# Keys and values of heads 4 to 7 projected in pairs; gates' logits split between VectorE and ScalarE

## The chip, the cores and the metric

The kernel runs on one core of a Trainium2 chip. The metric is the device time of one execution in microseconds (us), smaller is better. Besides the times there is one profiled execution, whose trace records every instruction of the engines: PE (TensorE, with its weight loads as PEld), DVE (VectorE), ACT (ScalarE), POOL (GpSimd), and SP, which only issues DMAs.

## The reference

One step of a decoder layer for 512 prompt tokens behind 16 meta tokens, and for 32 sample tokens (8 sequences of 4) that have 512 past keys and values each in a paged cache. All data are float32.

```python
h = rmsnorm(x, g_pre)
q, k, v, ga, cb, cc, ch, gc, ma, mc = jnp.split(h @ w_in, split_offsets(), axis=-1)
a = attend(q, k, v, b_sb) * jax.nn.silu(ga)          # 8 heads of 128, strictly causal
c = cb * causal_conv(cc * ch, w_conv, b_conv) * jax.nn.silu(gc)
m = jax.nn.sigmoid(ma + b_gate[:D]) * (a @ w_pa) + jax.nn.sigmoid(mc + b_gate[D:]) * (c @ w_pc)
y = x + rmsnorm(m @ w_out, g_post)
# attend: z = q.k / sqrt(128) + b;  A[t,s] = sigmoid(z_ts) * prod over s<j<t of (1 - sigmoid(z_tj))
```

The outputs also hold all keys, values and the convolution's last rows.

## The kernel before, in words

**Numbers in two parts.** Each float32 matrix is split into a part cast to the type fp32r and the rest (`hi`, `lo`), and each product is three matmuls: hi·hi, hi·lo, lo·hi. For weights ACT makes the cast (`whi`, line 240) and DVE subtracts it (`wlo`, line 241), 128x1024 at a time. A weight tile `raw` is one 512 KB load, issued by SP into five buffers; whi and wlo have three.

**Tokens.** 560 tokens (528 of the prompt with meta, 32 of the sample) lie along the free dimension of `h_hi`, `h_lo`, in two halves of 280 columns (272 where meta tokens aren't needed, 274 in the convolution's inputs).

**Two ways to project.** `proj` (line 271, its matmuls on line 256) takes one block of 128 output columns: 16 blocks of the contraction, three matmuls each, for both halves. `pair` with `seven` (lines 974 to 1024, matmuls on line 971) takes two blocks of output columns at once as a 2x2 block product with seven products of 8 blocks in place of eight. It needs sums of weight blocks (`s`, `w21`, on DVE), sums of token blocks (`t_hi`, `t_lo` 0 to 2, and `r1`, written over the block of h in the upper contraction half and second token half), and differences of partial results (`s2`, `s5`, `c`). Single projections that read h whole must come before that overwriting.

**The order.** Normalization and the first four queries; `head_now` for heads 0 to 3 (K, V, a query projection of head 4 to 7, and the prompt's attention); `head_later` for heads 4 to 7 (K and V by single projections, kept in DRAM for attention later); the block sums; then pairs: 4 for the attention's gate GA, 16 for the convolution (four groups of CC, CH, GC, CB), 16 for the gates MA and MC; then the products with w_pc with the attention of heads 4 to 7, with w_pa, and with w_out.

**The decode.** A generator, `decode_steps` (line 759), is advanced by `dec_step` and holds the sample's attention over the cache. Its first phase makes the logits: 16 units (half of the heads, sequence), each with two loads of query rows, broadcast to all partitions (`qb`, 512 KB), and four pages of keys (`kpage`, 256 KB), issued by POOL. A page takes 16 reduces on DVE, a product of 128 elements summed into one column of `z_all` each (line 781), 4 tokens by 4 heads. The first 6 units (`DEC1`) are spread over heads 0 to 7 ("part"), the other 10 over the first 25 pairs ("logits"), a step of `dec_group` (line 900) behind each pair being one page in the convolution and up to four in the gates. Then come the softplus and the sums over positions (`dec2`), and the values' pages in the last pairs.

**Who sets the order.** The tile framework schedules each engine's instructions by a simulated timeline with the program's order as priority, puts in the semaphores, and keeps the order of those that are marked (`pin`). Each engine then runs its own list strictly in order. Pools marked `side="right"` share one stack of SBUF, which bounds what can be held at once.

Of the kernel before, what the change touches and what calls it, by code (L numbers as in the profile page):

```python
# [17 lines left out]
P = 128  # L18
# [29 lines left out]
DEC1 = 6  # L48
# [12 lines left out]
def hybrid_step_kernel(  # L61
# [499 lines left out]
    def k_proj(h):  # L561
        o = proj(GATE_K + h * P, ALL)
        kr = hp.tile([P, T], F32, name="raw", bufs=2)
        for ob, s in nparts(o):
            act.copy(kr[:, s], ob)
# [11 lines left out]
    def v_proj(h, pl=None):  # L577
        o = proj(GATE_V + h * P, ALL)
        vr = hp.tile([P, T], F32, name="raw", bufs=2)
        for ob, s in nparts(o):  # L580
            act.copy(vr[:, s], ob)
# [5 lines left out]
        if pl is None:  # L587
            pool.dma_start(vn_scr[h][0:512].rearrange("(a p) d -> p a d", p=P), vn[:, 0:4, :])
            pool.dma_start(vn_scr[h][512:TP], vn[0:16, 4, :])
            return None  # L590
        return v_split(pl, vn)
# [126 lines left out]
    def head_now(h):  # L718
# [40 lines left out]
    def decode_steps():  # L759
# [3 lines left out]
        for said, part in (("part", units[:DEC1]), ("logits", units[DEC1:])):  # L763
            with tc.tile_pool(name="dec1", bufs=2, side="right") as d1:
                for hf, b in part:
# [3 lines left out]
                    for i in range(2):  # L769
                        qt = d1.tile([P, 2, 512], F32, name="qb", bufs=3)  # L770
# [3 lines left out]
                    for pg in range(NPG):  # L774
                        kt = d1.tile([P, 512], F32, name="kpage", bufs=3)
                        first(page_load(kt, kc, b, pg, cs))
                        for i, qt in enumerate(qts):
                            for t in range(2):
                                for h in range(4):
                                    junk = d1.tile([P, P], F32, name="junk", bufs=2)  # L780
                                    dve.tensor_tensor_reduce(  # L781
# [716 lines left out]
```

## Time and profile before

| | us |
|---|---|
| median of 3 runs (lowest to highest) | 1584.69 (1582.47 to 1585.42) |
| the profiled execution's own time | 1584.74 |
| its span, from the first instruction to the last | 1583.1 |
| single projections on line 256, share of the chain that ended last | 27.3% |
| pairs on line 971, share of that chain (into mm, into o) | 32.0%, 23.6% |

In the views that follow, "x" stands before a count, "mean ns" is the duration of one instruction with whatever it overlaps, and "idle before" the time in which its engine stood before it with the releaser named. Matmuls overlap: their durations are longer than the time from one to the next. The granted clock is TensorE's, as a share of full speed.

### The profile page before, as it was taken

The numbers are of one execution on the slowest core, as the hardware profiler recorded it, in microseconds if no ns is written. First come the engines' busy times: TensorE is split into PE (matmuls) and PEld (weight loads), VectorE is DVE, ScalarE is ACT, GpSimd is POOL, SyncE is SP. The second block draws the span as 40 slices with busy tenths as digits, with TensorE's granted clock in tenths as the row PEclk, the third lists the DMA queues.
The fourth block names the chain that finished last, engine by engine and source line by source line (L and its number), as shares of the span: only waits on it lengthen the run. The fifth ranks groups of instructions, "written<-read, shape, count | busy, mean of one in ns | idle before, by whom it ended". The sixth has DMA issues, their size and how long they took to land.

```text
span 1583.1 us, 32334 instructions
## 1 busy us (share of the span) xinstructions
PE 1560.7 (99%) x12172; PEld 1527.5 (96%) x12172; DVE 1268.5 (80%) x3574; ACT 761.7 (48%) x1345; POOL 234.7 (15%) x428
## 2 busy tenths in 40 slices
PE   8999999999999999999999999999999999999997
PEld 7999999999999999999999999898899999999997
DVE  7329999956799999999999997565678857877776
ACT  6245555435444444444444457444476734345552
POOL 1123333222111010011011102312100010000000
PEclk9999999999999999999999999999999999999999
DMA  8245556344454544445465545767595455433345
GB/s 263 82 137 186 168 160 184 107 130 136 150 180 124 151 130 140 146 134 162 120 181 173 162 138 168 245 194 226 157 306 172 148 178 165 152 107 94 101 143 183
DMA packets 300674, 252.77 MB, mean 160 GB/s; under 512 B 11521, under 2 KB 268613, under 8 KB 299701
## 3 DMA queue, kind: packets, MB, share of 16 engines
q1 hardware_dynamic: 272021, 160.45, 35.1%
q0 software_dynamic: 28368, 89.98, 17.0%
q8 instruction: 95, 1.56, 0.4%
q14 instruction: 62, 0.51, 0.1%
q10 hardware_dynamic: 128, 0.27, 0.1%
HBM read 217.95 MB, written 32.71 MB: 158 GB/s over the span
## 4 chain that ended last, share of the span: by engine, by line
PE 94%; DVE 2%; ACT 1%; DMA 1%; issue 1%; DVEq 0%; SPq 0%; ACTq 0%
PE mm L971 32%; PE mm L256 27%; PE o L971 24%; PE mm L321 2%; PE z L702 1%; PE o L714 1%; PE z L321 1%; PE tp L856 1%; DMA raw<-in_w_in 1%; PE z L620 1%; PE z L1439 1%; PE tp L505 0%; PE z L1293 0%; DVE wlo L241 0%; DMA at<-a_scr 0%
## 5 line engine op out<-in xcount | busy, mean ns | idle before, releaser
L240 ACT CAST whi<-raw 128x1024 fp32r<-128x1024 f32 x247 | 259.4, 1051 | 375.5 <-PE mm L971 135.0
L241 DVE TENSOR_TENSOR wlo<-raw,whi 128x1024 fp32r<-128x1024 f32 x247 | 301.7, 1222 | 90.2 <-ACT whi L240 88.0
L971 PE MATMUL mm<-h_hi,whi 128*128 128x272 f32 (+1 forms) x1152 | 333.5, 289 | 0.7 <-ACT whi L240 0.7
L971 PE MATMUL mm<-h_hi,wlo 128*128 128x272 f32 (+1 forms) x1152 | 332.6, 290 | 0.0
L971 PE MATMUL mm<-h_lo,whi 128*128 128x272 f32 (+1 forms) x1152 | 332.5, 289 | 0.0
L971 PE MATMUL o<-t_hi,whi 128*128 128x272 f32 (+1 forms) x864 | 251.6, 291 | 3.3 <-DVE c L997 3.3
L971 PE MATMUL o<-t_lo,whi 128*128 128x272 f32 (+1 forms) x864 | 251.2, 291 | 0.0
L971 PE MATMUL o<-t_hi,wlo 128*128 128x272 f32 (+1 forms) x864 | 251.1, 291 | 0.0
L781 DVE CUSTOM_DVE_ANT_0 junk<-kpage,qb 128x128 f32<-128x128 f32 x1024 | 246.0, 287 | 4.0 <-DMA qb<-q_scr 3.7
L971 PEld LDWEIGHTS mm<-h_hi,whi 128*128 128x128 f32 x1152 | 217.4, 189 | 6.1 <-ACT whi L240 3.5
L971 PEld LDWEIGHTS mm<-h_lo,whi 128*128 128x128 f32 x1152 | 216.8, 188 | 0.9 <-issue 0.8
L971 PEld LDWEIGHTS mm<-h_hi,wlo 128*128 128x128 f32 x1152 | 217.0, 189 | 0.2
L240 ACT CAST whi<-s 128x1024 fp32r<-128x1024 f32 x126 | 132.0, 1048 | 151.2 <-PE mm L971 48.5
L241 DVE TENSOR_TENSOR wlo<-s,whi 128x1024 fp32r<-128x1024 f32 x126 | 154.2, 1224 | 62.8 <-ACT whi L240 61.3
L256 PE MATMUL mm<-h_lo,whi 128*128 128x280 f32 (+1 forms) x640 | 187.6, 293 | 0.0
L256 PE MATMUL mm<-h_hi,wlo 128*128 128x280 f32 (+1 forms) x640 | 187.1, 293 | 0.0
L256 PE MATMUL mm<-h_hi,whi 128*128 128x280 f32 (+1 forms) x640 | 186.7, 292 | 0.0
L971 PEld LDWEIGHTS o<-t_hi,whi 128*128 128x128 f32 x864 | 164.1, 190 | 4.0 <-DVE c L997 4.0
L971 PEld LDWEIGHTS o<-t_hi,wlo 128*128 128x128 f32 x864 | 164.5, 190 | 0.9 <-issue 0.8
L971 PEld LDWEIGHTS o<-t_lo,whi 128*128 128x128 f32 x864 | 164.8, 191 | 0.0
L256 PEld LDWEIGHTS mm<-h_lo,whi 128*128 128x128 f32 x640 | 120.3, 188 | 0.8
L256 PEld LDWEIGHTS mm<-h_hi,wlo 128*128 128x128 f32 x640 | 120.5, 188 | 0.5
(452 smaller groups left out, 3166.7 us busy)
## 6 DMA issues: line engine op xcount, KB each, us to landing
raw<-in_w_in SPq DMA_DIRECT2D x192, 512.0 KB, 4.5
kpage<-in_cache_k POOLq DMA_DIRECT2D x64, 256.0 KB, 3.8
qb<-q_scr POOLq DMA_DIRECT2D x32, 512.0 KB, 5.7
vpage<-in_cache_v POOLq DMA_DIRECT2D x64, 256.0 KB, 5.7
raw<-in_w_out SPq DMA_DIRECT2D x32, 512.0 KB, 4.0
gate_scr<-g POOLq DMA_DIRECT2D x32, 272.0 KB, 4.9
gt<-gate_scr POOLq DMA_DIRECT2D x16, 544.0 KB, 4.5
raw<-in_w_pc SPq DMA_DIRECT2D x16, 512.0 KB, 4.7
```

The costliest lines, as they stand in the source:

```text
L240: act.copy(hi, x)
L241: dve.tensor_sub(lo, x, hi.bitcast(F32))
L256: pe.matmul(o, lhsT=w, rhs=r[:, t0:t1], start=(k == 0 and n == 0), stop=(k == nk - 1 and n == 2))
L321: pin(pe.matmul(o, lhsT=l, rhs=r[:, k, t0:t1], start=(start and m == 0), stop=(stop and m == 2), skip_group_check=True))
L620: pe.matmul(zt[:m, c0:c0 + n], lhsT=l[:, s0:s0 + m], rhs=r[:, ts:ts + n], start=(c0 == 0 and i == 0), stop=(i == 2), skip_group_check=True)
L702: pe.matmul(o, lhsT=l, rhs=x, start=False, stop=(i == len(ops) - 1), skip_group_check=True)
L714: pe.matmul(ot[:, ts - NMETA:ts - NMETA + n], lhsT=l[:m, st, :], rhs=x[:m, c0:c0 + n], start=False, stop=(g == GROUPS[-1] and i == 2), ski ...
L781: dve.tensor_tensor_reduce(out=junk, in0=kt[:, h * P:(h + 1) * P], in1=qt[:, t, h * P:(h + 1) * P], scale=1.0, scalar=0.0, op0=ALU.mult, o ...
L856: pin(pe.matmul(po[32 * j:32 * (j + 1), :], lhsT=lhs, rhs=rhs, start=(pg == 0), stop=last and n >= len(vts) - 4, tile_position=(0, 32 * j) ...
L971: pe.matmul(o, lhsT=l[:, k, :], rhs=r, start=(start and k == 0 and m == 0), stop=(stop and k == 7 and m == 2), skip_group_check=True)
L1439: pin(pe.matmul(o, lhsT=(m1, m2)[h][:, k + 8 * (q == 1), ts], rhs=two[h][q == 2][:, :, k, :], start=(n == 0), stop=(n == 47)))
```

## The change

Four edits that belong together.

1. K and V of heads 4 to 7 go through `pair`: K of heads 4 and 5, V of 4 and 5, K of 6 and 7, V of 6 and 7, each 280 columns wide (`heads_later`). The query projections of heads 4 to 7 leave `head_now` and stand behind head 3.
2. The block sums are made 280 wide. Those that need only the normalized tokens (`r1`, `x1`) come right behind the normalization, `y1` and the splits around the four query projections, and the overwriting of h, pinned on DVE, behind the last of them.
3. Of the 16 units of logits, 2 are left among heads 0 to 2, with two buffers for pages and query rows, and 14 go to 28 pairs, from the second K or V pair to the fifth of the gates. A `tick` behind each product advances them by a quarter of a page.
4. In these 14 units a page's first token is reduced on DVE as before (4 reduces). For the other three DVE makes products alone, one instruction of 512 elements and one of 1024, into `kq1` and `kq2` (one buffer each), and ACT sums them, 12 ACTIVATEs with an accumulator. DVE's reduces and products are pinned.

```diff
-DEC1 = 6
+DEC1 = 2
...
+    def k_out(hp, h, kr, qs):
...
         zz = z_ps()[0:TS, 0:TS]
-        pe.matmul(zz, lhsT=kr[:, TP:T], rhs=qs_all[:, h, :], start=True, stop=True)
+        pe.matmul(zz, lhsT=kr[:, TP:T], rhs=qs, start=True, stop=True)
...
+    def v_out(hp, h, vr):
...
         qr = hp.tile([P, TQ], F32, name="qr", bufs=2)[:, 0:PQ]
         nc.sync.dma_start(qr, qt_scr[h][:, 0:PQ])
         khi, klo = k_split(np_, k_proj(h))
-        dec_step(1 if h else 0, "part")
+        qhi, qlo = q_split(np_, qr)
+        dec_step((1, 8, 8, 0)[h], "part")
         vhi, vlo = v_proj(h, np_)
-        dec_step(1, "part")
-        q_proj(NOW + h)
-        dec_step(2, "part")
-        ot = next(attend(np_, h, khi, klo, vhi, vlo, *q_split(np_, qr)))
-        dec_step(2, "part")
-        at = np_.tile([P, PQ], F32, name="at", bufs=1)
+        dec_step((4, 8, 64, 0)[h], "part")
+        ot = next(attend(np_, h, khi, klo, vhi, vlo, qhi, qlo))
+        at = np_.tile([P, PQ], F32, name="lA", bufs=1)
         act.copy(at, ot)
         pool.dma_start(a_scr[h], at)
-    def head_later(h):
-        pool.dma_start(k_scr[h], k_proj(h))
-        dec_step(2, "part")
-        v_proj(h)
-        dec_step(2, "part")
+    def heads_later(h, qs):
+        for c, out in ((GATE_K, "k"), (GATE_V, "v")):
+            raws = [hp2.tile([P, T], F32, name="raw", bufs=2) for _ in range(2)]
+            seen = []
+            for m, half, b in pair(c + h * P, HC):
+                act.copy(raws[m][:, NMETA + half * HQ:NMETA + (half + 1) * HQ], b[:, HM:])
+                act.copy(raws[m][:, half * HM:(half + 1) * HM], b[:, :HM])
+                seen.append(m)
+                if seen.count(m) < 2:
+                    continue
+                if out == "k":
+                    pool.dma_start(k_scr[h + m], raws[m])
+                    k_out(hp2, h + m, raws[m], qs[:, h + m - NOW, :])
+                else:
+                    vn = v_out(hp2, h + m, raws[m])
+                    pool.dma_start(vn_scr[h + m][0:512].rearrange("(a p) d -> p a d", p=P), vn[:, 0:4, :])
+                    pool.dma_start(vn_scr[h + m][512:TP], vn[0:16, 4, :])
+            dec_group()
...
                     for i in range(2):
-                        qt = d1.tile([P, 2, 512], F32, name="qb", bufs=3)
+                        qt = d1.tile([P, 2, 512], F32, name="qb", bufs=2 if said == "part" else 3)
                         r0 = b * DT + 2 * i
                         first(pool.dma_start(qt, q_scr[r0:r0 + 2, cs].unsqueeze(0).broadcast_to([P, 2, 512])))
                         qts.append(qt)
                     for pg in range(NPG):
-                        kt = d1.tile([P, 512], F32, name="kpage", bufs=3)
+                        kt = d1.tile([P, 512], F32, name="kpage", bufs=2 if said == "part" else 3)
                         first(page_load(kt, kc, b, pg, cs))
-                        for i, qt in enumerate(qts):
-                            for t in range(2):
-                                for h in range(4):
-                                    junk = d1.tile([P, P], F32, name="junk", bufs=2)
-                                    dve.tensor_tensor_reduce(
-                                        out=junk, in0=kt[:, h * P:(h + 1) * P], in1=qt[:, t, h * P:(h + 1) * P],
-                                        scale=1.0, scalar=0.0, op0=ALU.mult, op1=ALU.add,
-                                        accum_out=z_all[:, pg, b, 4 * hf + h, 2 * i + t:2 * i + t + 1])
+                        if pg == 0 and (hf, b) == part[0]:
+                            yield
+                        def z_at(h, t):
+                            return z_all[:, pg, b, 4 * hf + h, t:t + 1]
+                        def direct(t):
+                            for h in range(4):
+                                junk = d1.tile([P, P], F32, name="junk", bufs=2)
+                                pin(dve.tensor_tensor_reduce(
+                                    out=junk, in0=kt[:, h * P:(h + 1) * P], in1=qts[t // 2][:, t % 2, h * P:(h + 1) * P],
+                                    scale=1.0, scalar=0.0, op0=ALU.mult, op1=ALU.add, accum_out=z_at(h, t)))
+                        if said == "part":
+                            for t in range(DT):
+                                direct(t)
+                                yield
+                            continue
+                        def times(kq, i, t0):
+                            qt = qts[i][:, t0:].rearrange("p t (h d) -> p t h d", d=P)
+                            k4 = kt.rearrange("p (h d) -> p h d", d=P).unsqueeze(1).broadcast_to([P, 2 - t0, 4, P])
+                            pin(dve.tensor_mul(kq, qt, k4))
+                        def act_sums(kq, t):
+                            for h in range(4):
+                                act.activation(kq[:, h], kq[:, h], AF.Copy, accum_out=z_at(h, t))
+                        direct(0)
+                        yield
+                        kq1 = d1.tile([P, 1, 4, P], F32, name="kq1", bufs=1)
+                        times(kq1, 0, 1)
+                        act_sums(kq1[:, 0], 1)
+                        yield
+                        kq2 = d1.tile([P, 2, 4, P], F32, name="kq2", bufs=1)
+                        times(kq2, 1, 0)
+                        act_sums(kq2[:, 0], 2)
+                        yield
+                        act_sums(kq2[:, 1], 3)
                         yield
             yield said
...
     def dec_group():
         n = n_group[0] = n_group[0] + 1
-        if n <= 25:
-            dec_step((0, 2, 2, 2)[n - 1] if n <= 4 else 1 if n <= 20 else 4, "logits")
-        else:
-            dec_step(2 if n in (26, 28) else 1)
+        if n == 1:
+            dec_step(1, "logits")
+        elif n == 29:
+            dec_step(64, "logits")
+        elif n > 29:
+            dec_step(2 if n in (30, 32) else 1)
+    def dec_tick():
+        if 1 <= n_group[0] < 29:
+            dec_step(1, "logits")
...
     for h in range(NOW):
         q_proj(h)
-    for h in range(NOW):
-        head_now(h)
-    nctx.close()
-    for h in range(NOW, H):
-        head_later(h)
-    dec_step(64, "part")
...
+    ysum = ExitStack()
+    with tc.tile_pool(name="tsum", bufs=1, side="right") as tsp:
+        r1, x1 = (tsp.tile([P, 8, HC], F32, name=n) for n in ("r1", "x1"))
+        def part(x, *ij):
+            return (blk(x, *ij) if ij else x)[:, c:c + 2]
         for c in range(0, 8, 2):
-            def part(x, *ij):
-                return (blk(x, *ij) if ij else x)[:, c:c + 2]
-            r, x, y = part(r1), *(tsp.tile([P, 2, HU], F32, name=n) for n in "xy")
+            r, x = part(r1), part(x1)
             dve.tensor_sub(r, part(h_f, 0, 0), part(h_f, 0, 1))
             dve.tensor_add(r, r, part(l_f, 0, 0))
             dve.tensor_sub(r, r, part(l_f, 0, 1))
             dve.tensor_add(x, r, part(h_f, 1, 1))
             dve.tensor_add(x, x, part(l_f, 1, 1))
-            t_split(part(t_hi[0]), part(t_lo[0]), x)
+        for h in range(NOW):
+            head_now(h)
+        y1 = ysum.enter_context(tc.tile_pool(name="ysum", bufs=1, side="right")).tile([P, 8, HC], F32, name="y1")
+        for h in range(NOW, H):
+            q_proj(h)
+        for c in range(0, 8, 2):
+            x, y = part(x1), part(y1)
             dve.tensor_sub(y, part(h_f, 0, 0), x)
             dve.tensor_add(y, y, part(l_f, 0, 0))
-            t_split(part(t_hi[1]), part(t_lo[1]), y)
+        nctx.close()
+        tctx = ExitStack()
+        t_hi, t_lo = [], []
+        for i in range(3):
+            ttp = tctx.enter_context(tc.tile_pool(name=f"tt{i}", bufs=1))
+            t_hi.append(ttp.tile([P, 8, HC], F32R, name=f"t_hi{i}"))
+            t_lo.append(ttp.tile([P, 8, HC], F32R, name=f"t_lo{i}"))
+        for c in range(0, 8, 2):
+            x = part(x1)
+            t_split(part(t_hi[0]), part(t_lo[0]), x)
             dve.tensor_sub(x, part(h_f, 1, 0), x)
             dve.tensor_add(x, x, part(l_f, 1, 0))
-            t_split(part(t_hi[2]), part(t_lo[2]), x)
         for c in range(0, 8, 2):
-            t_split(blk(h_hi, 0, 1)[:, c:c + 2], blk(h_lo, 0, 1)[:, c:c + 2], r1[:, c:c + 2])
+            t_split(part(h_hi, 0, 1), part(h_lo, 0, 1), part(r1), pin)
+        for i, src in ((1, y1), (2, x1)):
+            for c in range(0, 8, 2):
+                t_split(part(t_hi[i]), part(t_lo[i]), part(src))
+        ysum.close()
     hctx.close()
...
@@ -980,29 +1035,37 @@
         sums = sums or (lambda m: tmp("c"))
         x, q, y = mm_ps()[:, :n], mm_ps()[:, :n], o_ps()[:, :n]
         product(x, w_split(w11), rb(0, 0), True, False)
+        tick()
         dve.tensor_add(s, w21, w22)
         product(q, w_split(s), rb(0, 1), True, False)
+        tick()
         act.activation(y, x, AF.Copy, scale=-1.0)
         dve.tensor_add(s, s, w11)
         product(y, w_split(s), rt(0), False, False)
...
         dve.tensor_sub(c12, q, s2)
         yield 0, 1, c12
         product(y, w_split(w22), rt(2), False, True)
+        tick()
         yield 1, 0, y
+        tick()
...
         def rt(i):
-            return lambda k: (t_hi[i][:, k, HU - n:HU], t_lo[i][:, k, HU - n:HU])
+            return lambda k: (t_hi[i][:, k, HC - n:], t_lo[i][:, k, HC - n:])
...
-        yield from seven(ws, n, rb, rt, s, lambda name: sp2.tile([P, HU], F32, name=name)[:, :n])
+        yield from seven(ws, n, rb, rt, s, lambda name: sp2.tile([P, HC], F32, name=name)[:, :n], tick=dec_tick)
...
+    with tc.tile_pool(name="heads2", bufs=1) as hp2:
+        qs = hp2.tile([P, H - NOW, TS], F32, name="qs")
+        for h in range(NOW, H):
+            pool.dma_start(qs[:, h - NOW, :], qt_scr[h][:, PQ:TQ])
+        for h in range(NOW, H, 2):
+            heads_later(h, qs)
...
-                after = hl[0].tile([P, P], F32, name="after")
-                dve.tensor_scalar_add(after, neg_u.bitcast(F32), 1.0)
                 loaded = head_loads(NOW, hl[0])
     dec_step(64)
     d3ctx.close()
     hs0 = hlctx.enter_context(tc.tile_pool(name="split0", bufs=1, side="right"))
+    after = hs0.tile([P, P], F32, name="after")
+    dve.tensor_scalar_add(after, neg_u.bitcast(F32), 1.0)
```

More of the change, by code (lines that the diff above doesn't have):

```diff
@@ L559, in v_split, with raw_of @@
         return vhi, vlo
-    def k_proj(h):
-        o = proj(GATE_K + h * P, ALL)
-        kr = hp.tile([P, T], F32, name="raw", bufs=2)
+    def raw_of(o):
+        raw = hp.tile([P, T], F32, name="raw", bufs=2)
         for ob, s in nparts(o):
-            act.copy(kr[:, s], ob)
+            act.copy(raw[:, s], ob)
+        return raw
+    def k_out(hp, h, kr, qs):
         kn = hp.tile([P, 5, P], F32, name="nat", bufs=2)
@@ L571, in k_proj @@
         zz = z_ps()[0:TS, 0:TS]
-        pe.matmul(zz, lhsT=kr[:, TP:T], rhs=qs_all[:, h, :], start=True, stop=True)
+        pe.matmul(zz, lhsT=kr[:, TP:T], rhs=qs, start=True, stop=True)
         act.activation(z_new[:, :, h, :], zz.rearrange("p (b t) -> p b t", t=DT), AF.Identity,
                        bias=bsb[0:TS, h:h + 1])
-        return kr
[L577 to L581, printed above, removed]
+    def k_proj(h):
+        kr = raw_of(proj(GATE_K + h * P, ALL))
+        k_out(hp, h, kr, qs_all[:, h, :])
+        return kr
+    def v_out(hp, h, vr):
         vn = hp.tile([P, 5, P], F32, name="nat", bufs=2)
@@ L972, in product, with seven @@
                           stop=(stop and k == 7 and m == 2), skip_group_check=True)
-    def seven(ws, n, rb, rt, s, tmp, sums=None):
+    def seven(ws, n, rb, rt, s, tmp, sums=None, tick=lambda: None):
         w11, w21, w22, w12 = ws
@@ L1004, in seven @@
         product(y, w_split(w22), rt(2), False, True)
+        tick()
         yield 1, 0, y
+        tick()
     def blocks_of(src, c):
```

24 lines of the change are left out of this document (8 added, 16 removed).

## The prediction

> **What bounds the kernel now.** The page first: engines' shares and the chain that ended last.
>
> ```profile
> span 1583.1 us, 32334 instructions
> PE 1560.7 (99%) x12172; PEld 1527.5 (96%) x12172; DVE 1268.5 (80%) x3574; ACT 761.7 (48%) x1345; POOL 234.7 (15%) x428
> PE 94%; DVE 2%; ACT 1%; DMA 1%; issue 1%; DVEq 0%; SPq 0%; ACTq 0%
> ```
>
> TensorE is the bound: it is busy throughout and the chain hardly leaves it. Since matmuls overlap, its busy share doesn't say whether it runs at its pace, so next comes the count by windows (columns: window, length, then busy time and count of PE, PEld, DVE, ACT, POOL; granted clock, DMA share, GB/s).
>
> ```profile
> 60.00:80.00 20.00, 20.00 (x151) 20.00 (x150) 3.86 (x5) 3.79 (x7) 4.20 (x8) 1.00 0.35 92
> ...
> 307.00:360.00 53.00, 53.00 (x416) 52.37 (x416) 31.65 (x46) 20.46 (x42) 11.97 (x20) 1.00 0.39 115
> 420.00:440.00 20.00, 18.23 (x133) 18.02 (x132) 18.37 (x71) 7.72 (x11) 2.24 (x4) 0.91 0.47 143
> 440.00:460.00 20.00, 20.00 (x160) 20.00 (x160) 19.31 (x75) 8.93 (x14) 3.62 (x6) 1.00 0.51 157
> 541.00:626.30 85.30, 85.30 (x677) 85.25 (x677) 81.60 (x262) 36.58 (x56) 7.92 (x14) 1.00 0.46 137
> 862.40:904.70 42.30, 42.30 (x338) 42.30 (x337) 40.41 (x149) 20.05 (x28) 5.11 (x9) 1.00 0.56 169
> ```
>
> From 440 us on, 160 matmuls stand in 20 us, 0.125 us each: packed. But DVE is at 96% in one conv group (four pairs, 541 to 626) and 96% in two gate pairs (862 to 905). So what leaves TensorE is won in full; what is put on DVE or ACT in these stages may turn into a stall.
>
> **Products of heads 4 to 7.** One head's K or V costs 2 halves x 16 x 3 = 96 matmuls of 280 columns; a pair costs 7 products x 8 x 3 = 168 in place of 192. Eight singles were 768 matmuls, four pairs are 672: 96 fewer. Their pace is in the chain, in a stretch of single projections.
>
> ```profile
> 293.58 10.03 PE mm L256 x78
> ...
> 413.97 9.92 DMA raw<-in_w_in
> ```
>
> 10.03 / 78 = 0.1286 us, so 96 x 0.1286 = **-12.3 us**. All of it is on the chain. Weight loads and bytes stay the same (four raw tiles for two heads either way).
>
> **DVE: logits.** Widths decide here. The timeline gives issue-to-issue paces, the groups by form give durations.
>
> ```profile
> 484.25 0.29 DVE L781 CUSTOM_DVE_ANT_0 junk<-kpage,qb 128x128 f32<-128x128 f32 x1
> 484.47 0.08 DVE L781 DVE_READ_ACCUMULATOR2_ANT z_all<- 128x1 f32 x1
> 484.47 0.29 DVE L781 CUSTOM_DVE_ANT_0 junk<-kpage,qb 128x128 f32<-128x128 f32 x1
> ...
> 486.00 1.23 DVE L241 TENSOR_TENSOR wlo<-s,whi 128x1024 fp32r<-128x1024 f32 x1 [0.18 <-ACT whi L240]
> 487.15 0.29 DVE L781 CUSTOM_DVE_ANT_0 junk<-kpage,qb 128x128 f32<-128x128 f32 x1
> ```
>
> ```profile
> L495 DVE TENSOR_TENSOR qlo<-qr,qhi 128x512 fp32r<-128x512 f32 x8 | 5.4, 679 | 11.3 <-ACT qhi L494 11.3
> ```
>
> A reduce takes 0.215 us; a page of the key cache had 16, 3.4 us. Now it has 4 reduces (0.86), one product of 512 elements (0.68 less the 0.08 by which instructions overlap: 0.60) and one of 1024 (1.15): 2.6 us. No row has a product with a broadcast page; the nearest are these tensor-tensor rows of equal size, and I take them. But the pages get denser in time: two for each pair. How many stood there, by the windows of line 781 alone (each reduce counts two):
>
> ```profile
> 126.00:305.00 179.00, 90.76 (x756) 1.00 0.53 161
> ...
> 541.00:626.30 85.30, 22.71 (x182) 1.00 0.46 137
> 862.40:904.70 42.30, 14.58 (x122) 1.00 0.56 169
> ```
>
> Conv group: 81.6 - 91 x 0.215 = 62.0 of other work, + 8 pages x 2.6 = 82.8 of 85.3 us: 97%, as before. Two gate pairs: 40.4 - 61 x 0.215 + 4 x 2.6 = 37.7 of 42.3: better than before. So DVE's sum alone costs nothing.
>
> **ACT: sums.** Each page adds 12 ACTIVATEs of 128 elements, each with an accumulator read. The nearest rows are the output stage's squares.
>
> ```profile
> 1439.91 0.26 ACT L1286 ACTIVATE sq<-z 128x128 f32<-128x128 f32 x1
> 1440.07 0.19 ACT L1286 ACTIVATION_READ_ACCUMULATOR sq<-z 128x1 f32 x1
> 1440.29 0.28 ACT L1286 ACTIVATE sq<-z 128x128 f32<-128x128 f32 x1
> ```
>
> ```profile
> L1286 ACT ACTIVATE sq<-z 128x128 f32<-128x128 f32 x60 | 16.5, 275 | 14.9 <-PE z L1293 14.0
> L985 ACT ACTIVATE o<-mm 128x272 f32<-128x272 f32 x35 | 13.4, 382 | 7.0 <-PE mm L971 7.0
> L1286 ACT ACTIVATION_READ_ACCUMULATOR sq<-z 128x1 f32 x62 | 12.0, 194 | 0.0
> L494 ACT CAST n<-gt 128x272 fp32r<-128x272 f32 x24 | 10.0, 418 | 13.5 <-DVE gt L1247 8.0 <-DVE gt L1250 5.2 <-DVE gt L1253 0.3
> L506 ACT COPY nat<-tp 128x512 f32<-128x512 f32 x16 | 9.4, 587 | 38.6 <-PE tp L505 38.5
> ```
>
> ```profile
> L240 ACT CAST whi<-raw 128x1024 fp32r<-128x1024 f32 x8 | 8.4, 1052 | 13.9 <-PE mm L256 12.4 <-issue 1.5
> ...
> L565 ACT COPY raw<-mm 128x272 f32<-128x272 f32 x4 | 1.5, 384 | 3.3 <-PE mm L256 3.3
> ...
> L565 ACT COPY raw<-mm 128x8 f32<-128x8 f32 x4 | 0.7, 170 | 0.0
> ```
>
> One start to the next is 0.38 us out of PSUM; out of SBUF about 0.04 more (418 against 382 ns at 272 elements). Bounds 0.38 (the read overlaps) and 0.51 (275 + 36 + 194, no overlap); I take 0.40, near the pace that is seen. A pair has 24: 9.6 us. Conv group 36.6 + 38.4 = 75 of 85.3 (88%). Two gate pairs 20.05 + 19.2 = 39.3 of 42.3 (93%). K and V pairs (the last three rows, from the stretch 307 to 360): 7 casts of 1.05 less 0.10 of overlap (6.65), 3 partial results of 0.38 (1.14), 4 halves copied in two pieces of 0.38 and 0.17 (2.2), two naturals of 0.59, about 0.5 of small ones: 11.7, + 9.6 = 21.3 of 168 x 0.1286 = 21.6 us (99%), for three pairs, as the first has no logits. It fits everywhere, barely.
>
> [...] The trace shows a fixed cost (275 ns for 128 elements, 382 for 272), but also the overlap; what a missing overlap would make of the time is the second rival, by rows.
>
> **New waits.** The single-buffered products wait for ACT's sums of the page before, and ACT's sums for the products; the products are pinned in order on DVE, so behind a late one stand wlo, the sums of weights and the partial results, and behind these SP's weight loads (their buffers are freed by DVE) and TensorE. Unbounded by any row of its own. The nearest case is the one stall of the gates' stage: DVE, in order, waited for query rows, a weight load came late, TensorE starved.
>
> ```profile
> 417.26 0.29 DVE L781 CUSTOM_DVE_ANT_0 junk<-kpage,qb 128x128 f32<-128x128 f32 x1 [3.31 <-DMA qb<-q_scr]
> ```
>
> ```profile
> 428.76 0.39 PE L971 MATMUL o<-t_hi,whi 128*128 128x272 f32 x1 [1.76 <-DVE c L997]
> ```
>
> That window has 133 matmuls against 160: 27 x 0.125 = 3.4 us for a gap of 1.76, because the granted clock fell to 0.91 there. [...] I take one more such event for the whole stage, **+3.4 us**; bounds 0 and 19.6 (last rival). The event at 428 itself I leave in: the burst of three 512 KB query loads still opens the logits, now in the K and V pairs. Gone, it gives 3.4 back.
>
> **Moves.** Block sums, by the groups of DVE and ACT between 280 and 366 us:
>
> ```profile
> L934 DVE TENSOR_TENSOR h_lo<-r,h_hi 128x548 fp32r<-128x548 f32 x4 | 2.9, 722 | 0.3 <-ACT h_hi L933 0.2
> ...
> L945 DVE TENSOR_TENSOR r<-r,h_lo 128x548 f32<-128x548 f32 x4 | 2.7, 710 | 0.0
> ```
>
> The first 20 instructions, 0.64 us each with overlap (13 us), go to where DVE has 3.9 us in 20; 32 more (20.5 us) stand beside four Q projections (48 us of TensorE, 9 of DVE) and the first pair. The last splits wait for the last Q product; the first product of the first pair (24 x 0.1286 = 3.1 us) doesn't need them, and a first chunk, a cast and a difference, takes about 1.4. Nothing, as now. If that cover fails, about 3 us, once. POOL's queue: the outputs of heads 4 to 7 now stand among page loads; with three buffers pages are loaded two ahead, 21 us. DMA: two pages for a pair is the density of 862 to 905 (share 0.56), where TensorE lost nothing. Heads 0 to 3 lose their interleaved Q, see the third rival, but also most of their reduces: 378 in 179 us become 128. Taken as nothing.
>
> **Sum.** The profiled execution took 1584.74 us (span 1583.1 and 1.6 around it), the median of three 1584.69. 1584.7 - 12.3 + 3.4 = **1575.8 us**.
>
> **Rivals.** (1) No new stall, and the one at 428 goes: 1584.7 - 12.3 - 3.4 = 1569.0. For it: DVE was at 96% before and TensorE packed. 0.20. (2) ACT becomes the bound, at 0.51 a sum: 12.1 a pair; gate and silu pairs up to 22.1 against 21.15, nine of them, up to +9; K and V pairs 23.8 against 21.6, three, +6.6: 1584.7 - 12.3 + 15.6 = 1588.0. At 0.45 only the K and V pairs are over, by 0.9: 1575.1. Against it: the read starts at 1440.07, before its ACTIVATE ends at 1440.17. 0.10. (3) The attention's chain comes out from under the projections.
>
> ```profile
> 160.98 0.35 PE L620 MATMUL z<-qhi,khi 128*128 128x400 f32 x1
> ```
>
> ```profile
> 199.17 0.40 PE L714 MATMUL o<-hiA,vlo 128*128 128x512 f32 x1
> ```
>
> ```profile
> 207.02 0.34 PE L620 MATMUL z<-qhi,khi 128*128 128x400 f32 x1
> ```
>
> From first score to last output 38.6 us, in a period of 46.0. Without a Q projection (96 x 0.126 = 12.1) the period is 33.9: 4.7 short, three times, +14.1: 1586.5. Against it: 20 us of reduces stand in that chain's way today and mostly leave. 0.10. (4) Slower: DVE in the conv groups. Of 85.3 us DVE idles 3.7 now, partly for whi; its new work leaves 2.5. With ACT at 88% instead of 43% a cast comes later. If DVE's waits double to 7.4, each group runs 4.9 over, four groups +19.6: 1592.0. It decides from 5.6 us of waits a group (3.1 over, times four, eats the 12.3). Against it: before, the waits were partly mere slack. 0.15. My forecast has the remaining 0.45.
>
> **Chances and range.** A measurement of this kernel can tell about 0.2%, 3.2 us. Faster (below 1581.5): rival 1, nearly all of my case, half of rival 2: 0.67. Same: 0.16, from the rest of 2 and 3. Slower: 0.17, rival 4 and a rest. The range goes from 1567 to 1588: it leaves out most of rival 4 and little below.
>
> **What would show it.** Right: 96 matmuls fewer; TensorE at 160 in 20 us in the conv groups; ACT at 85 to 93% there; an accumulating ACTIVATE each 0.40 us. Wrong: gaps on PE in each group with wlo behind a product that waits for an ACT sum (rival 4), whi behind sums (2), PE idle before the second product of attention between 110 and 240 us (3), or an end of the logits so late that it stands in the softplus stage.

## The result, and the profile after

| | before | after |
|---|---|---|
| median of 4 runs each (lowest to highest), us | 1583.58 (1582.13 to 1585.42) | 1600.22 (1597.74 to 1600.62) |
| ratio, 95% interval | | 1.0101 [1.0084, 1.0119] |
| profiled execution's span, us | 1583.1 | 1598.8 |

The changed kernel is 1% slower; 1575.8 was forecast, and the range ended at 1588. From the page of the changed kernel:

```profile
span 1598.8 us, 32298 instructions
PE 1560.4 (98%) x12076; PEld 1520.6 (95%) x12076; DVE 1257.7 (79%) x2378; ACT 962.9 (60%) x2711; POOL 244.9 (15%) x432
PE 84%; DVE 7%; ACT 4%; issue 3%; DMA 2%; POOL 1%; DVEq 0%; SPq 0%; ACTq 0%; POOLq 0%
```

The 96 matmuls are gone (12172 to 12076), but the chain now leaves TensorE for 16% of the span. Where: the count by windows, first of before, then of after (columns as in the prediction).

```profile
240.00:300.00 60.00, 60.00 (x457) 58.26 (x456) 58.13 (x309) 26.64 (x54) 17.84 (x34) 1.00 0.47 145
...
460.00:820.00 360.00, 359.18 (x2842) 358.76 (x2840) 345.86 (x1118) 156.58 (x236) 35.69 (x62) 1.00 0.49 143
```

```profile
240.00:300.00 60.00, 49.16 (x352) 47.63 (x351) 40.03 (x54) 27.93 (x50) 8.24 (x18) 0.89 0.25 74
460.00:820.00 360.00, 354.45 (x2751) 348.28 (x2750) 337.53 (x648) 259.98 (x1004) 42.96 (x74) 1.00 0.51 149
...
548.00:637.00 89.00, 87.50 (x681) 85.94 (x680) 84.12 (x161) 64.18 (x248) 10.46 (x18) 1.00 0.52 150
```

Two stages lost matmuls. Around the first pair of K, 457 - 352 = 105, or 13.5 us at 0.1286. In the convolution's pairs 2842 - 2751 = 91, or 11.5 us at 360/2842 = 0.127 each; a group of four pairs, 677 matmuls in 85.3 us before, now has 681 in 89. For the whole span I summed an **excess**: the distance from each matmul's start to the next, less the median for its shape. It is 51.4 us before and 80.1 after. By stage the difference is +13.9 (240 to 300), +11.4 (460 to 820) and +3.4 for the rest (+3.9 before 240, +1.3 from 300 to 460, -5.3 from 820 to 1180, +3.6 behind); with the 12.3 us of products saved that makes +16.4, and the spans differ by 15.7.

**The first stall.** The timeline of the changed kernel, engine by engine, around the first pair (start, length, engine, line, operation, then idle before and its releaser):

```profile
254.44 0.59 ACT L730 COPY lA<-o 128x512 f32<-128x512 f32 x1 [3.63 <-PE o L715]
...
259.19 2.35 ACT L968 CAST t_hi<-x 128x560 fp32r<-128x560 f32 x4 [4.03 <-DMA a_scr<-lA]
...
275.63 1.04 ACT L240 CAST whi<-s 128x1024 fp32r<-128x1024 f32 x1 [3.14 <-DVE s L1039]
```

```profile
259.89 1.40 DVE L969 TENSOR_TENSOR t_lo<-x,t_hi 128x560 fp32r<-128x560 f32 x2 [8.03 <-ACT t_hi L968]
...
271.72 2.69 DVE L969 TENSOR_TENSOR h_lo<-r,h_hi 128x560 fp32r<-128x560 f32 x4
274.33 1.22 DVE L1039 TENSOR_TENSOR s<-raw 128x1024 f32<-128x1024 f32 x1
...
277.90 1.22 DVE L241 TENSOR_TENSOR wlo<-s,whi 128x1024 fp32r<-128x1024 f32 x1
```

```profile
276.73 0.60 PE L1026 MATMUL mm<-h_hi,whi 128*128 128x280 f32 x1 [9.23 <-ACT whi L240]
279.18 0.60 PE L1026 MATMUL mm<-h_hi,wlo 128*128 128x280 f32 x1 [1.61 <-DVE wlo L241]
```

The block sums' halves lie in memory that attention's pool gives back. ACT's first cast of t_hi waits 4.03 us until head 3's output, copied into that pool at 254.44, has left for DRAM; DVE stands 8.03 us behind it, then works off its row of halves and sums for 14 us before it reaches `s`, the sum of weight blocks that the second product needs. TensorE stands 9.23 us, and then runs at half clock (columns: window, length, busy time and count of PE, PEld, DVE, ACT, POOL; granted clock, DMA share, GB/s):

```profile
267.20:271.50 4.30, 0.30 (x2) 0.09 (x1) 4.30 (x8) 1.78 (x4) 1.07 (x2) 1.00 0.18 71
271.60:285.20 13.60, 6.86 (x28) 6.53 (x29) 12.24 (x14) 4.36 (x5) 3.76 (x7) 0.50 0.34 96
285.30:300.00 14.70, 14.70 (x117) 14.70 (x116) 9.77 (x10) 6.25 (x13) 0.54 (x1) 1.00 0.39 112
```

**The convolution.** No single stall, but many of 0.2 to 0.8 us, mostly at like places of each group. One of them, around 597 us, by the timeline of ACT, DVE and PE:

```profile
593.96 0.30 ACT L815 ACTIVATE kq<-kq 128x128 f32<-128x128 f32 x1
...
595.13 1.04 ACT L240 CAST whi<-s 128x1024 fp32r<-128x1024 f32 x1
```

```profile
592.74 0.68 DVE L811 TENSOR_TENSOR kq<-qb,kpage 128x512 f32<-128x512 f32 x1
593.34 1.22 DVE L1043 TENSOR_TENSOR s<-s,raw 128x1024 f32<-128x1024 f32 x1
...
594.98 1.42 DVE L1139 TENSOR_SCALAR cv<-u,wcv 128x512 f32<-128x512 f32 x4
596.32 0.74 DVE L1142 SCALAR_TENSOR_TENSOR cv<-u,wcv,cv 128x512 f32<-128x512 f32 x1
596.98 1.22 DVE L241 TENSOR_TENSOR wlo<-s,whi 128x1024 fp32r<-128x1024 f32 x1
```

```profile
597.17 0.39 PE L1026 MATMUL mm<-h_hi,whi 128*128 128x272 f32 x1 [0.28 <-ACT whi L240]
598.25 0.40 PE L1026 MATMUL o<-t_hi,wlo 128*128 128x272 f32 x1 [0.45 <-DVE wlo L241]
```

The sum `s` is there at 594.56, behind a product; its cast starts 0.57 us later, behind four of ACT's sums. The high half is there at 596.17, but the low half starts 0.8 us later, behind convolution work that this product doesn't need. TensorE starts at 597.17 on the next weight, whose cast is done at 597.12, and then stands again until this low half is there. So I also measured this **delay**, from the end of each whi to the start of its wlo, as a mean over the weights of 460 to 820 us (100 to 118, and 70 in e11): 0.69 us before, 1.43 after. By what DVE ran in between, products take 0.36 of the rise and other weights' sums and low halves 0.39; direct tokens take 0.11 less.

The delay shows only the low halves, though. In this stage TensorE waits longer for high halves than for low ones (total, times, longest):

```profile
PE mm L1026 <- ACT whi L240: 2.5, 7, 0.4
PE o L1026 <- DVE wlo L241: 1.5, 3, 0.6
PE o L1026 <- ACT whi L240: 0.9, 4, 0.2
```

The other place that comes back in every group (531, 620, 709 and 798 us) has the sum of weights itself late, behind a product on DVE; the cast follows it after 0.08 us:

```profile
616.59 0.68 DVE L811 TENSOR_TENSOR kq<-qb,kpage 128x512 f32<-128x512 f32 x1
...
617.89 1.21 DVE L1043 TENSOR_TENSOR s<-s,raw 128x1024 f32<-128x1024 f32 x1
```

```profile
619.18 1.03 ACT L240 CAST whi<-s 128x1024 fp32r<-128x1024 f32 x1
```

```profile
620.27 0.39 PE L1026 MATMUL o<-t_hi,whi 128*128 128x272 f32 x1 [0.23 <-ACT whi L240]
```

### The profile page after: what moved, and what is told of

The parts are those of the page before. It is cut to its first block, busy times and chain, and to the rows that moved or that the text cites. A ratio compares the mean times of both kernels' runs of the same rounds, so it can differ in the third digit from the quotient of the medians.

```text
span 1598.8 us, 32298 instructions
## 1 busy us (share of the span) xinstructions
PE 1560.4 (98%) x12076; PEld 1520.6 (95%) x12076; DVE 1257.7 (79%) x2378; ACT 962.9 (60%) x2711; POOL 244.9 (15%) x432
## 4 chain that ended last, share of the span: by engine, by line
PE 84%; DVE 7%; ACT 4%; issue 3%; DMA 2%; POOL 1%; DVEq 0%; SPq 0%; ACTq 0%; POOLq 0%
PE mm L1026 32%; PE o L1026 23%; PE mm L256 18%; PE mm L321 2%; DVE wlo L241 2%; PE z L321 1%; PE tp L899 1%; PE z L703 1%; ACT whi L240 1%; PE o L715 1%; DVE junk L798 1%; ACT kq L815 1%; DVE kq L811 1%; DMA raw<-in_w_in 1%; PE z L1508 1%
## 5 line engine op out<-in xcount | busy, mean ns | idle before, releaser
L1026 PE MATMUL mm<-h_hi,whi 128*128 128x272 f32 (+2 forms) x1280 | 374.1, 292 | 14.5 <-ACT whi L240 12.1
L1026 PE MATMUL mm<-h_hi,wlo 128*128 128x272 f32 (+2 forms) x1280 | 373.5, 292 | 2.0 <-DVE wlo L241 1.6
L1026 PE MATMUL mm<-h_lo,whi 128*128 128x272 f32 (+2 forms) x1280 | 371.5, 290 | 0.0
L1026 PE MATMUL o<-t_hi,whi 128*128 128x272 f32 (+2 forms) x960 | 279.3, 291 | 1.4 <-ACT whi L240 0.9
L1026 PE MATMUL o<-t_hi,wlo 128*128 128x272 f32 (+2 forms) x960 | 278.3, 290 | 1.5 <-DVE wlo L241 1.5
L1026 PE MATMUL o<-t_lo,whi 128*128 128x272 f32 (+2 forms) x960 | 277.4, 289 | 0.0
L1026 PEld LDWEIGHTS mm<-h_hi,wlo 128*128 128x128 f32 x1280 | 242.6, 190 | 4.0 <-DVE wlo L241 3.7
L815 ACT ACTIVATE kq<-kq 128x128 f32<-128x128 f32 x672 | 198.8, 299 | 50.5 <-DVE kq L811 50.1
L815 ACT ACTIVATION_READ_ACCUMULATOR kq<-kq 128x1 f32 x672 | 126.6, 188 | 0.0
L811 DVE TENSOR_TENSOR kq<-qb,kpage 128x512 f32<-128x512 f32 x112 | 106.4, 950 | 0.0
```

The costliest lines, as they stand in the source:

```text
L811: pin(dve.tensor_mul(kq, qt, k4))
L815: act.activation(kq[:, h], kq[:, h], AF.Copy, accum_out=z_at(h, t))
L1026: pe.matmul(o, lhsT=l[:, k, :], rhs=r, start=(start and k == 0 and m == 0), stop=(stop and k == 7 and m == 2), skip_group_check=True)
```

## The experiments

All change the changed kernel. "Matmuls" and "DVE" are count and busy time in the window 460 to 820; the excess is that of the two stages. Each ratio is to the kernel before as it ran beside that run (medians of 1582.5 to 1584.1).

| run | median us | ratio to before [95%] | excess 240-300, 460-820 | matmuls | DVE | delay |
|---|---|---|---|---|---|---|
| before | 1583.58 | | 1.2, 1.7 | 2842 | 345.9 | 0.69 |
| after | 1600.22 | 1.0101 [1.0084, 1.0119] | 15.1, 13.1 | 2751 | 337.5 | 1.43 |
| e1_at | 1591.64 | 1.0054 [1.0035, 1.0072] | 9.8, 12.8 | 2755 | 339.0 | 1.42 |
| e2_split | 1596.57 | 1.0079 [1.0053, 1.0105] | 15.1, 13.0 | 2752 | 337.8 | 1.42 |
| e3_nosums | 1596.62 | 1.0091 [1.0061, 1.0121] | 13.9, 9.3 | 2783 | 339.8 | 1.23 |
| e4_direct | 1585.55 | 1.0018 [1.0007, 1.0030] | 14.8, 1.1 | 2847 | 346.6 | 0.58 |
| e5_short | 1610.85 | 1.0187 [1.0170, 1.0204] | 13.8, 22.6 | 2663 | 339.3 | 1.58 |
| e6_even | 1617.39 | 1.0223 [1.0195, 1.0251] | 13.7, 24.2 | 2624 | 326.3 | 1.46 |
| e7_direct_at | 1579.87 | 0.9983 [0.9974, 0.9993] | 9.6, 0.4 | 2854 | 347.0 | 0.65 |
| e8_direct_split_at | 1583.10 | 1.0004 [0.9995, 1.0014] | 11.8, 1.2 | 2848 | 346.4 | 0.61 |
| e9_unpin | 1650.65 | 1.0408 [1.0381, 1.0434] | 10.1, 53.9 | 2425 | 313.6 | 1.27 |
| e10_pinwlo | 1696.20 | 1.0710 [1.0691, 1.0729] | 14.6, 52.0 | 2424 | 297.3 | 3.21 |
| e11_pinall | 1995.08 | 1.2593 [1.2568, 1.2618] | 15.1, 141.2 | 1713 | 212.3 | 2.24 |
| e12_short_nosums | 1611.51 | 1.0181 [1.0165, 1.0196] | 14.0, 22.8 | 2675 | 341.6 | 1.72 |
| e14_direct_sums | 1626.45 | 1.0273 [1.0248, 1.0297] | 13.8, 26.4 | 2647 | 339.8 | 0.95 |
| e15_tick_late | 1598.99 | 1.0093 [1.0073, 1.0113] | 14.8, 13.0 | 2752 | 338.1 | 1.46 |
| e13_later | 1575.92 | 0.9956 [0.9942, 0.9969] | 7.6, 1.3 | 2846 | 346.1 | 0.61 |

### The stall in front of the first pair

```diff
 e1_at
-        at = np_.tile([P, PQ], F32, name="lA", bufs=1)
+        at = hp.tile([P, 5, P], F32, name="nat", bufs=2)[:, 0:4, :]  # head 3 only, flattened
 e2_split
+    npk = nctx.enter_context(tc.tile_pool(name="nowk", bufs=2))   # ahead of np_; khi, klo, qhi, qlo
```

> The changed kernel, with the output of head 3's attention copied to a buffer of the heads' pool instead of the memory that the new block sums' halves take over; nothing else differs. Theory T (the first pair of K stands still because the halves wait until that output has left the chip, a 3.77 us transfer and the copy before it): the vector engine's wait of 8.03 us behind the cast of t_hi shrinks to about 4, the 9.49 us gap of TensorE at 267 to about 5, and the median goes from 1600.2 to 1594-1597. Rival U (the gap is set by the last Q projection and the row of rewritten halves of h behind it, the memory only happens to be late as well): gap and median stay, 1599-1602.

> The changed kernel, with the halves of K and Q of heads 0 to 3 in a pool of their own, first in the memory, so that the halves of the first block sum wait only for head 3's scores (216-220 us) and not for its whole attention (254 us); nothing else differs. Theory T: the casts of t_hi come before the attention's end, the gap of 9.49 us at 267 goes to under 2 and with it the half clock from 272 to 285; the median falls by 8 to 14, to 1586-1592. Rival U (last Q projection and the rewritten halves of h): the gap falls by less than 3, the half clock stays, 1596-1601.

Theory T held for e1_at, with more than it had forecast: 8.6 us from one buffer, 5.3 of them in this stage (15.1 to 9.8). For e2_split it failed as I put it: 3.7 us, and the excess stays, as rival U had it. Its ACT timeline says why:

```profile
266.01 0.59 ACT L730 COPY lA<-o 128x512 f32<-128x512 f32 x1 [4.09 <-PE o L715]
...
269.70 2.34 ACT L969 CAST t_hi<-y 128x560 fp32r<-128x560 f32 x4 [1.99 <-DMA a_scr<-lA]
```

```profile
270.39 2.70 DVE L970 TENSOR_TENSOR t_lo<-y,t_hi 128x560 fp32r<-128x560 f32 x4 [8.26 <-ACT t_hi L969]
```

The first sum's halves came early, but the second's now wait for the same transfer, and DVE idles 8.26 us behind them. And with other dependences the planner put Q projections ahead of head 3's attention: its output is copied at 266.0 in place of 254.4.

e7 and e8 repeat both edits on e4_direct (below); e13 adds to e7 that the second and third sums are formed in the steps between the first pair's products.

```diff
 e13_later, on e7_direct_at (excerpt)
-        for i, src in ((1, y1), (2, x1)):
-            for c in range(0, 8, 2):
-                t_split(part(t_hi[i]), part(t_lo[i]), part(src))
+        def later():   # advanced by dec_tick in the first pair; y in a tile of hp
+            for i in (1, 2):
+                for c in range(0, 8, 2):
...
+                    t_split(t_hi[i][:, s], t_lo[i][:, s], y)
+                    if c in (2, 6):
+                        yield
```

> All four tokens direct on VectorE (as the run that gave 1585.6) and the output of head 3's attention in the heads' pool (as the run that gave 1591.6 in place of 1600.2). If the two costs are separate the gains add: 1585.6 - 8.6 = 1577.0, 1575-1580, faster than before (1582.5). If both were the same stall seen twice, 1584-1587.

> As the run before, and with the halves of K and Q of heads 0 to 3 in a pool of their own, so that the first block sum's halves wait for nothing of the attention. With the halves in place but the output left in the old memory the wait only moved to the second sum's halves (8.26 us, on the same transfer): 1596.6. Theory T (the memory's release, for every one of the three sums): the gaps that the other run still has at 267 to 274 (2.13 and 4.69) shrink to under 3 together, 1571-1576. Rival V (those 6.8 are VectorE's row of halves and sums in front of the first weight's half, not a wait): they stay, 1575-1580.

> The fastest so far (all tokens direct, output of head 3's attention in the heads' pool; 1579.9), with the second and third block sum and their halves spread over the first pair of K instead of standing ahead of it: in front of the pair remain the first sum's halves and the rewritten halves of h. Theory T2 (the 2.13 and 4.69 us at 267 to 274 and the half clock behind them, 9.6 of excess, are VectorE's row of halves and sums in front of the first weight's low half): excess at 240-300 falls to under 4, median 1573-1577. Rival V (the sums are late anyway and the stall moves to the fifth product of the pair): 1577-1582.

The gains of e1 and e4 do not add fully: 1579.9, not 1577.0. What adds is the stage (14.8 to 9.6, 5.2 as in e1); the other 3 of e1 lay elsewhere. The interval, 0.9974 to 0.9993, still leaves out 1. e8 is slower than e7: the copy of head 3's output, at 254.11 in e7's ACT timeline, stands at 266.45, so theory T is not all of it. That the planner's order makes the rest is likely, but no run changed this order alone.

```profile
254.11 0.59 ACT L733 COPY nat<-o 128x512 f32<-128x512 f32 x1 [3.63 <-PE o L715]
```

```profile
266.45 0.59 ACT L733 COPY nat<-o 128x512 f32<-128x512 f32 x1 [4.09 <-PE o L715]
```

e13 has the time that T2 said, 1575.9, but not for T2 alone: the stage's excess fell from 9.6 to 7.6, where under 4 was expected, and 2.1 more came from other stages. Its page and windows:

```profile
span 1572.1 us, 32235 instructions
PE 1547.1 (98%) x12076; PEld 1513.9 (96%) x12076; DVE 1301.1 (83%) x3610; ACT 778.7 (50%) x1372; POOL 246.2 (16%) x432
```

```profile
240.00:300.00 60.00, 55.80 (x414) 53.87 (x413) 44.14 (x58) 31.55 (x58) 10.61 (x22) 0.97 0.34 103
...
460.00:820.00 360.00, 359.31 (x2846) 358.84 (x2845) 346.09 (x1117) 156.67 (x237) 36.29 (x63) 1.00 0.48 142
```

What is left of the stage's excess, 6.4 over before's, again comes from DVE's row of halves and block sums: a sum of weights stands late in it (its cast waits for it and ends at 271.25, and TensorE starts right behind), then a low half, and slow matmuls follow (0.23 us from start to start from 274.38 on; granted clock 0.92 in 275 to 290):

```profile
268.96 1.22 DVE L1059 TENSOR_TENSOR s<-s,raw 128x1024 f32<-128x1024 f32 x1
```

```profile
270.21 1.04 ACT L241 CAST whi<-s 128x1024 fp32r<-128x1024 f32 x1 [0.48 <-DVE s L1059]
```

```profile
271.36 0.37 PE L1042 MATMUL o<-t_hi,whi 128*128 128x280 f32 x1 [2.61 <-issue]
272.26 0.40 PE L1042 MATMUL mm<-h_hi,whi 128*128 128x280 f32 x1 [0.41 <-ACT whi L241]
273.98 0.60 PE L1042 MATMUL o<-t_hi,wlo 128*128 128x280 f32 x1 [1.18 <-DVE wlo L242]
```

Its total excess is 53.0, 1.6 over before's; 1.6 - 12.3 = -10.7, and the spans differ by -11.0. This version beats both kernels.

### The convolution's 11 us

```diff
 e3_nosums
-                                act.activation(kq[:, h], kq[:, h], AF.Copy, accum_out=z_at(h, t))
 e4_direct
-                        if said == "part":          # all pages: four direct tokens
+                        if True:
 e5_short
-                            pin(dve.tensor_mul(kq, qt, k4))
+                            for h in range(4):
+                                pin(dve.tensor_mul(kq[:, :, h], qt[:, :, h], k1))
 e6_even
-                        times(kq1, 0, 1); ...; times(kq2, 1, 0)
+                        for t in (1, 2, 3):  # a product of 512, its sums, a step
```

> The changed kernel without the sums on ScalarE: the products of three tokens in four are still formed on VectorE but not summed, so these logits are left at zero. ScalarE loses 12 sums of 0.30 us a page, 8 pages a conv group: 29 us of the 64 busy in 89. Theory D (a conv group takes 89 in place of 85.5 because bunches of products and direct logits on VectorE make the halves of the weights late; ScalarE has room): groups stay at 88-89 and the median within 4 of 1600.2 (1596-1601). Rival A (ScalarE's casts of the weights wait behind the sums): groups go back to 85-86, the median to 1583-1590.

> The changed kernel with all four tokens of a page direct on VectorE (16 of 0.212 us, 3.39 us a page in place of 2.59), at the same places, and no sums on ScalarE. Theory D: 8 pages a conv group are 6.4 us more of VectorE, 83.4 to about 90, which fills the group; groups 92-95, the median 1612-1628. Rival A (ScalarE's sums cost the time): groups 85-89 and 1585-1598.

> The changed kernel with each product of VectorE cut into four, one for a head: four of 128 and four of 256 elements in place of one of 512 (0.602 us) and one of 1024 (1.135 us); the sums on ScalarE stay. About 0.2 and 0.32 us each by the 0.212 of a direct token, so a page costs some 2.9 in place of 2.59. All direct, 3.39 a page, gave 1585.6, without sums 1596.6, so neither VectorE's share nor the sums alone is the cause. Theory L (an instruction of 1.135 us that a half of a weight waits behind): conv groups go to 85-87 and the median to 1588-1594, in spite of more work on VectorE. Rival C (the chain product, sums, next product across the two engines, with one buffer each, whatever its pieces): median 1597-1604.

> The changed kernel with the 1024-element product cut by token: every step of a page has its own product of 512 elements and its own four sums, three buffers of one size, so the load is 0.85, 0.60, 0.60, 0.60 us a step in place of 0.85, 0.60, 1.14, 0. Theory L (the length of the longest piece): about half of what short pieces bring, 1592-1597. Rival C (product and sums chained across engines): as changed, 1597-1603. If it is below 1590, unevenness of the steps was the cause.

Theory D, too much of VectorE, falls: with all tokens direct DVE does more (346.6 in 360 us against 337.5) and hardly anything is late. Rival A, ScalarE's sums, explains a small part: without them 9.3 of the 13.1 are left. Theory L, the length of an instruction, falls twice: with short pieces the excess is 22.6, with even ones 24.2. Both times lie above every range I had given, rival C's too, so rival C is not settled by them.

```diff
 e12_short_nosums: e5_short and e3_nosums together
 e14_direct_sums, on e4_direct
+                                    act.activation(kq1[:, h], kt[:, h * P:(h + 1) * P], AF.Copy, accum_out=zz1[:, h:h + 1])
 e9_unpin
-  pin(dve.tensor_mul(...)), pin(dve.tensor_tensor_reduce(...))
+  dve.tensor_mul(...), dve.tensor_tensor_reduce(...)
 e10_pinwlo: pin(dve.tensor_sub(lo, x, hi)) in w_split; e11_pinall: s and w21 as well
 e15_tick_late
-        product(q, w_split(s), rb(0, 1), True, False)
-        tick()
+        w = w_split(s)
+        tick()
+        product(q, w, rb(0, 1), True, False)
```

> The changed kernel with the products in four pieces each and without the sums on ScalarE (logits of three tokens in four stay at zero): nothing waits for a product, and VectorE has only short pieces. With sums the pieces gave 1610.9, whole products without sums 1596.6. Theory L (a long instruction ahead of a weight's half): conv excess falls from 9.3 to under 4, median 1586-1592. Rival O (where the planner puts the products, whatever their length): excess stays 8 or more, 1595-1605.

> All tokens direct on VectorE, and beside them twelve sums a page on ScalarE as in the changed kernel, but over the page of keys itself, so that they wait for no product (their results are not used). Without them 1585.6. Rival A2 (12 sums of 0.30 us a page in ScalarE's row make the high halves late by themselves): conv excess rises from 1.1 to 5 or more, 1590-1598. Rival C (they cost only where they wait for a product in the row ahead of a cast): excess under 3, 1584-1589.

> The changed kernel with the order of the logits' instructions on VectorE left to the kernel's planner again (products and direct tokens not held in the order of the program); nothing else differs. In the conv stage a weight's low half starts 1.43 us after its high half is there (mean of 114), 0.58 with all tokens direct, 0.69 before. Theory O (the planner puts the low halves behind the products; the order, not the load, makes them late): if the held order is what prevents better places, the mean delay falls below 1 and the median to 1588-1594. Rival C (the sums on ScalarE in its queue ahead of the casts, waiting for their products): delay and median stay, 1597-1604.

> The changed kernel with the low halves of the weights held in the program's order among the logits' instructions on VectorE, from the second pair on: behind one low half comes one step of logits, then the next low half, so no low half can fall behind more than one step. Theory O: the delay of low behind high halves falls from 1.43 to under 1, the excess of the conv stage from 13 to under 6, the median to 1588-1595. Rival C (sums in ScalarE's queue): high halves are late, not low ones; the excess stays above 9, 1597-1604.

> As the run before, with the sums of weight blocks held in that order too: VectorE then follows the program for all that TensorE waits on, and only the conv's own work floats. Theory O: as the run before or better, 1586-1594. If the program's order is worse than the planner's for these sums (a sum waits for a weight's load and holds the row behind it), slower than the run before by over 3.

> The changed kernel with each step of the logits set, in the program, behind the halves of the next block of weights instead of ahead of them (between a split and its product, not after the product); same instructions. Theory O (the place in VectorE's row is what costs, and the planner gives an earlier place to what stands earlier in the program): low halves start under 1.1 us after the high ones in place of 1.43, the conv stage's excess falls from 13.1 to under 7, the median to 1588-1595. If the planner places by its own times and not by the program, the delay stays near 1.4 and the median at 1596-1604.

With short pieces the excess is 22.8 without the sums and 22.6 with them: there the sums cost nothing, the products all. In e14 the sums cost 25 in this stage, and 41 in the median, more than either rival had; but they waited for something else, as the list of ACT's waits in 460 to 820 us says (total, times, longest):

```profile
ACT kq L809 <- DMA kpage<-in_cache_k: 33.4, 20, 4.3
```

They stood in ACT's row ahead of casts before their page had landed. That run shows what a waiting sum costs, not what a ready one does; A2 stays untested.

What is shown is how much the rows' order weighs. e9 has the same instructions on every engine as the changed kernel and is 50 us slower; e10, again the same instructions, 96; e11, which holds the sums of weights as well, 395. All three went against my theory O in direction: neither leaving the order to the planner nor holding low halves in the program's order helped. e15 moved the steps in the program, and delay (1.46) and time (1599.0) stayed, as they would if the planner places them by its simulated times. In every kernel with products the delay is 1.2 us or more, in those with direct tokens alone, and before, 0.6 to 0.7. But it doesn't rank them: e9 has 1.27 at an excess of 53.9, the changed kernel 1.43 at 13.1, and it leaves out the sums and high halves that TensorE waits for most. **Open:** why the planner puts sums and low halves further back with products than with more direct work. That it does is seen in the traces; that this order, and not something else that comes with the products, costs the time is argued, since no run changed that place alone and won.

## Why the prediction was wrong, step by step

- **Products, -12.3.** Right: 96 matmuls fewer, and e13's span is 11.0 below before's with 1.6 of new excess.
- **Moves, "Nothing, as now. If that cover fails, about 3 us, once".** This step failed: 13.9 us. I asked when the last Q product ends and how long a first chunk takes, and the first product did follow without a gap. I didn't ask when the sums' memory comes free, nor what stands in DVE's row ahead of the weights' sums of the second product. Of the 13.9, one buffer carries 5.3 (e1_at), the second and third sum's place in the row 2.0 (e13); 6.4 are still there in e13, in the gaps on DVE's row shown above and the slow matmuls behind them, and no run took them away.
- **DVE's sum.** Right in size, wrong in what follows. I had 82.8 us a group; the group shown has 84.1, in 89. But e4 runs packed with more. That DVE's sum "alone costs nothing" was true; what cost, as I argue above, is the place of the work in the row, and I had no term for it.
- **New waits, +3.4.** The term that was mis-sized: 11.4. Its mechanism, products and sums waiting for each other, carries about the 3.8 that e3, which has no sums, takes away (13.1 to 9.3); the other part came with the products alone, and direct tokens (e4) take away all of it. Why is open, as said above. The event at 428 is gone (excess of 420 to 440: 3.5 before, 0 after), but 380 to 400 now has 3.6, and had none.
- **ACT's sums.** 0.40 taken; measured 0.295 from start to start, below my lower bound, since 0.09 of the read's 0.19 us run under the next sum:

```profile
586.43 0.30 ACT L815 ACTIVATE kq<-kq 128x128 f32<-128x128 f32 x1
586.63 0.19 ACT L815 ACTIVATION_READ_ACCUMULATOR kq<-kq 128x1 f32 x1
586.73 0.29 ACT L815 ACTIVATE kq<-kq 128x128 f32<-128x128 f32 x1
```

- **Rivals.** (2) Out as the bound: ACT is at 64 us of 89, though single casts stand behind sums (595 us above). (3) No stall of its size in the heads' stage (excess 17.3 against 13.4 before 240 us): Q projections filled in under the attention, but attention's end is what the sums' memory then waited for, so its price came later. (4) Nearest, in place and size: 19.6 forecast for the groups, 11.4 found. High halves did come later, as it said (TensorE waits 3.4 us for them there, 1.5 for low ones), but less from ACT's load than from sums of weights that DVE has late: without ACT's sums (e3) 9.3 of the 13.1 remain. The first stall was in no rival, and it decides: without its 13.9, -12.3 + 11.4 + 3.4 is +2.5, no change that could be told.

## What to carry to other kernels

When a step is moved, ask of its outputs which pool's memory they take and which last transfer frees it, and of each engine's row what now stands between that wait and the next weight: here DVE stood 8.03 us and then worked 14 us before it reached `s`. An engine's busy share doesn't tell whether work on it is late: here 96% of DVE was packed before, and 94% with the products lost 11 us. Where a planner orders the rows, an edit to one instruction's form can move others too, so try to measure the form and the order apart.

## What the runs showed of the hardware beyond that

The granted clock fell to 0.50 some 4.4 us into the first stall and stayed there until 285.2, 6 us past its last gap. Behind that gap 24 matmuls ran 0.233 us from start to start in place of 0.1286 (two of them below), so about 2.5 of the 13.9 us are slow matmuls, not idle time. In e13, with the gaps of 2.61, 0.41 and 1.18 us shown above, the window 240 to 300 has 0.97.

```profile
279.57 0.43 PE L1026 MATMUL mm<-h_hi,whi 128*128 128x280 f32 x1
279.81 0.43 PE L1026 MATMUL mm<-h_lo,whi 128*128 128x280 f32 x1
```
